# DMA transposes issued by ScalarE, and nine pairs of the first MLP's u tiles turned by them too

## The chip, the cores and the metric

One core of a Trainium2 chip runs the whole kernel. The metric is the device time of one execution in microseconds (us), as the median of several runs. The engines are TensorE (PE, with its weight loads PEld), VectorE (DVE), ScalarE (ACT), GpSimd (POOL) and SyncE (SP); each works through its own instructions in order and waits for the others by semaphores. A DMA is issued by an instruction on one engine's queue and carried out by the core's 16 DMA engines.

## The reference

A decoder trunk of two layers on 256 tokens of width 2048, in f32. Layer 0 mixes tokens by a convolution module, layer 1 by differential attention; each layer then has a squared-ReLU MLP of width 8192.

```python
def squared_relu_mlp(h, w1, b1, w2, b2):
    u = jnp.square(jax.nn.relu(h @ w1 + b1))
    return u @ w2 + b2
...
for i in range(DEPTH):
    mod = cond @ ada_w[i] + ada_b[i]
    sh_m, sc_m, g_m, sh_f, sc_f, g_f = [m[:, None, :] for m in jnp.split(mod, 6, axis=-1)]
    h = x * (1.0 + sc_m) + sh_m
    ...
    x = layer_norm(DEEPNORM_ALPHA * x + g_m * y, ln_mix_g[i], ln_mix_b[i])
    h = x * (1.0 + sc_f) + sh_f
    y = squared_relu_mlp(h, mlp_w1[i], mlp_b1[i], mlp_w2[i], mlp_b2[i])
    x = layer_norm(DEEPNORM_ALPHA * x + g_f * y, ln_ffn_g[i], ln_ffn_b[i])
```

In the attention, q and k are rotated (rope) after the product `h @ w_qkv`.

## The kernel before

**Products.** A product has the 128 tokens of a row half t (0 or 1) as its stationary side and a 512 wide strip of weights as its moving side. Every f32 value is split into a high part (a rounded copy) and a low part (the rest), and three matmuls stand for one: high by high (L702), high by low (L704), low by high (L705). A strip over 16 chunks of 128 input features is a *group*; its two row halves fill two PSUM banks. Weights arrive in tiles of 1 MB (`load_halves`, L638, SyncE's queue, four buffers `w_w`). Half of a tile, two chunks, is a *half tile*: ScalarE casts its high half `wh` (L657), VectorE subtracts to get the low half `wl` (L659), into four buffers each. One half tile feeds 12 matmuls, and a group has eight of them. `fetch` asks for half tiles four ahead (`AHEAD`), so a cast waits until TensorE has finished the half tile four places before.

**The MLP.** The width 8192 goes in four quarters q. Each quarter computes four groups g of `u` by the first weight matrix (names `w1_i_q_g`, i is the layer), then four groups by the second (`w2_i_q_n`), which take `u` as their stationary side. For that `u` must lie with features on the partitions, so each of its 512 wide tiles has to be turned. There are two ways, chosen by `by_dma(i, q, g)` for both row halves (a *pair*):

- By TensorE: ScalarE copies the PSUM bank to `us` (L1483), and two half tiles later (`U_WAIT`) four transposes per row half write `ut` (L1488). In layer 0 ScalarE adds the bias with Relu out of `ut` (L1494), four pieces per row half, and VectorE squares (L1499; in quarter 0 ScalarE, L1497); in layer 1 VectorE does both (L1501, L1504).
- By DMA (`halves_t`): ScalarE copies the bank into two planes of 16-bit halves `uh` (L1417), a DMA transposes them into `ux` (L1419), and after `T_WAIT[i]` half tiles ScalarE joins the planes to `r` (L1423); bias, Relu and square follow (L1428 on ScalarE and L1429 on VectorE in layer 0, L1431 and L1432 on VectorE in layer 1). `T_WAIT` is 6 for layer 0 and 4 for layer 1.

Both ways end in `put_split`, which makes `u_hi` (L515, ScalarE) and `u_lo` (L518, VectorE). Before the change, 13 pairs go by DMA, all in layer 1: quarters 1 to 3, and group 3 of quarter 0. The rest, 16 pairs of layer 0 and three of layer 1, go by TensorE.

**Rope.** `rope_evac` turns the rotated q and k tiles in the same manner: ScalarE makes the two planes (L1669), a DMA turns them (L1674), and four half tiles later ScalarE joins them into `qT` or `kT` (L1680). Seven pairs go this way, the last k group by TensorE (L1686).

**Beside it.** During layer 0's MLP, VectorE also computes layer 1's modulation: dot products of rows of `ada_w` with the condition (`adaw`, L230), whose 1 MB tiles share the four buffers of the weights.

**Order.** TensorE and VectorE keep the order in which the code is written. ScalarE's and SyncE's order in the MLPs and the attention is set by a scheduler, so a later step of one tile can stand ahead of an earlier step of another.

Of the kernel before, what the change touches and what calls it, by code (L numbers as in the profile page):

```python
# [82 lines left out]
def group_order(s):  # L83

    return list(range(NGRP))[::1 if (len(SLICES) - s) % 2 else -1]
# [72 lines left out]
def trunk(  # L158
# [8 lines left out]
    nc = tc.nc  # L167
# [16 lines left out]
    def tp_tile(name):  # L184
        return ps_tp[0].tile([P, 512], F32, tag="tp", name=name)
# [57 lines left out]
    def defer(n, fn):  # L243
        put_off.append((ticks[0] + n, fn))
# [265 lines left out]
    def put_split(pair, c0, n, s0, ns, src, eng=None, trail=False):  # L510

        hi, lo = pair
        h = hi[:, c0:c0 + n, s0:s0 + ns]
        l = lo[:, c0:c0 + n, s0:s0 + ns]
        nc.scalar.copy(h, src)  # L515

        def low():
            (eng or nc.vector).tensor_tensor(l, src, h.bitcast(F32), op=ALU.subtract)  # L518
        if trail:
            trailing.append(low)  # L520
        else:
            low()
# [739 lines left out]
    for s, (f0, nf) in enumerate(SLICES):  # L1262
# [6 lines left out]
        for pos, k in units:  # L1269
            g = group_order(s)[pos]  # L1270
# [3 lines left out]
            if (s, h) in X_AT:  # L1274
                a, b = X_AT[s, h]
# [8 lines left out]
            if nf > 1 or pos % 2 == 0:  # L1284
                parts = w_parts.pop(0)
# [14 lines left out]
            if not last and h >= END_AT[s]:  # L1300
                n = h - END_AT[s] - 1 + (s + 1 < BOTH_PE)
# [106 lines left out]
        defer(4 + q, lambda q=q: alpha_x(q))  # L1408

    def by_dma(i, q, g):  # L1410
        return i == 1 and (q > 0 or g == 3)

    def halves_t(t, ps, uT, i, q, g, n0):

        name = f"{i}_{q}_{g}_{t}"
        parts = work.tile([P, 2, NG], U16, tag="X", name=f"uh_{name}", bufs=3)
        nc.scalar.copy(parts, ps.bitcast(U16).rearrange("p (n b) -> p b n", b=2))  # L1417
        turned = work.tile([P, 2, 4, P], U16, tag="A", name=f"ux_{name}")
        nc.sync.dma_start_transpose(turned.rearrange("p b a n -> p (b a) n"), parts.rearrange("p b n -> p (b n)"))  # L1419

        def rest():
            r = work.tile([P, 4, P], F32, tag="B", name=f"r_{name}")
            nc.scalar.copy(r.rearrange("p a n -> p (a n)").bitcast(U16).rearrange("p (a n b) -> p a n b", a=4, b=2),  # L1423
                           turned.rearrange("p b a n -> p a n b"))
            f0 = i * 64 + n0 // P
            if i == 0:
                for j in range(4):
                    nc.scalar.activation(r[:, j, :], r[:, j, :], AF.Relu, bias=cv["b1c"][:, f0 + j:f0 + j + 1])  # L1428
                nc.vector.tensor_tensor(r, r, r, op=ALU.mult)  # L1429
            else:  # L1430
                nc.vector.tensor_tensor(r, r, cv["b1c"][:, f0:f0 + 4].unsqueeze(2).broadcast_to([P, 4, P]), op=ALU.add)  # L1431
                nc.vector.scalar_tensor_tensor(r, r, 0.0, r, ALU.max, ALU.mult)  # L1432
            put_split(uT, g * 4, 4, t * P, P, r, trail=True)
        defer(T_WAIT[i], rest)
# [218 lines left out]
    def rope_evac(nm, g, kv):  # L1653
        def on_t(t, ps):
            ph = ps.rearrange("p (h d) -> p h d", h=4)
            p1 = work.tile([P, 4, P], F32, tag="A", name=f"rp1_{nm}{g}{t}")
            nc.vector.tensor_tensor(p1.rearrange("p h (b d) -> p (h b) d", b=2),
                                    ps.rearrange("p (h d) -> p h d", d=64),
                                    at["cos"][:, t, :].unsqueeze(1).broadcast_to([P, 8, 64]), op=ALU.mult)
            p2 = work.tile([P, 4, P], F32, tag="B", name=f"rp2_{nm}{g}{t}")  # L1660
            nc.vector.tensor_tensor(p2[:, :, 0:64], ph[:, :, 64:128],
                                    at["sinN"][:, t, :].unsqueeze(1).broadcast_to([P, 4, 64]), op=ALU.mult)
            nc.vector.tensor_tensor(p2[:, :, 64:128], ph[:, :, 0:64],
                                    at["sinP"][:, t, :].unsqueeze(1).broadcast_to([P, 4, 64]), op=ALU.mult)
            nc.vector.tensor_tensor(p1, p1, p2, op=ALU.add)

            if (nm, g) != ("k", 3):
                parts = p2.rearrange("p h n -> p (h n)").bitcast(U16).rearrange("p (b n) -> p b n", b=2)
                nc.scalar.copy(parts, p1.rearrange("p h n -> p (h n)").bitcast(U16).rearrange("p (n b) -> p b n", b=2))  # L1669
                if t == 0:  # L1670
                    turned = late["pool"].tile([P, 2, 4, P], U16, tag="qkx", name=f"qkx_{nm}{g}{t}")
                else:
                    turned = work.tile([P, 2, 4, P], U16, tag="A", name=f"qkx_{nm}{g}{t}")
                nc.sync.dma_start_transpose(turned.rearrange("p b a n -> p (b a) n"),  # L1674
                                            parts.rearrange("p b n -> p (b n)"))

            def joined():
                if t == 0:
                    kv[nm] = work.tile([P, 4, S], F32, tag="X", name=f"{nm}T_{g}", bufs=3)
                nc.scalar.copy(kv[nm].bitcast(U16).rearrange("p h (n b) -> p h n b", b=2)[:, :, t * P:(t + 1) * P, :],  # L1680
                               turned.rearrange("p b h n -> p h n b"))

            def rest():
                pt = tp_tile(f"qkt_{nm}{g}{t}")
                for h in range(4):
                    nc.tensor.transpose(out=pt[:, h * P:(h + 1) * P], in_=p1[:, h, :], identity=ident)  # L1686
                if t == 0:
                    kv[nm] = work.tile([P, 4, S], F32, tag="X", name=f"{nm}T_{g}", bufs=3)
                nc.scalar.copy(kv[nm][:, :, t * P:(t + 1) * P], pt.rearrange("p (h n) -> p h n", h=4))
            if (nm, g) != ("k", 3):  # L1690
                defer(4, joined)
            else:
                defer(3, rest)
        return on_t
# [233 lines left out]
```

## Time and profile before

| | us |
|---|---|
| median of 3 runs (2267.3 to 2270.41) | 2267.64 |
| the profiled execution | 2264.22 |
| its span, first to last instruction | 2262.3 |
| TensorE's mean granted clock | 0.996 |
| DMA engines' mean busy share | 0.78 |
| mean rate of the DMA engines, GB/s | 274 |

The span falls into the convolution layer (to about 423 us), the first MLP (423 to 1070), attention with its projections (about 1100 to 1530) and the second MLP (to the end). Rows of a timeline give start, duration, engine, line, operation, output and inputs; in brackets, how long the engine stood idle before it and what ended that. A row of the group view gives busy time, mean ns of one, and after the bar the idle time before them. A matmul's row lasts longer than its place in the stream, because matmuls are pipelined: the distance between two starts is what one costs.

### The profile page before, as it was taken

The numbers are of one execution on the slowest core, as the hardware profiler recorded it, in microseconds if no ns is written. First come the engines' busy times: TensorE is split into PE (matmuls) and PEld (weight loads), VectorE is DVE, ScalarE is ACT, GpSimd is POOL, SyncE is SP. The second block draws the span as 40 slices with busy tenths as digits, with TensorE's granted clock in tenths as the row PEclk, the third lists the DMA queues.
The fourth block names the chain that finished last, engine by engine and source line by source line (L and its number), as shares of the span: only waits on it lengthen the run. The fifth ranks groups of instructions, "written<-read, shape, count | busy, mean of one in ns | idle before, by whom it ended". The sixth has DMA issues, their size and how long they took to land.

```text
span 2262.3 us, 28005 instructions
## 1 busy us (share of the span) xinstructions
PE 2223.8 (98%) x10900; PEld 1779.6 (79%) x10900; DVE 1713.5 (76%) x2124; ACT 1139.8 (50%) x1528; POOL 38.2 (2%) x53
## 2 busy tenths in 40 slices
PE   8999999999999999999999999999999999999999
PEld 5677657687888888888878788787888888888886
DVE  7688889778977888878878877887965665665567
ACT  4336773564355355355365555545444643643652
POOL 0000000000000000000000010100000000000000
PEclk9999999999999999999999999999999999999999
DMA  9996789699988888888858876875976765766773
GB/s 397 419 392 270 298 323 397 218 340 330 349 301 315 308 290 319 320 306 287 292 168 280 270 228 213 288 272 178 331 247 199 209 211 191 224 202 192 220 239 111
DMA packets 259712, 619.04 MB, mean 274 GB/s; under 512 B 52623, under 2 KB 52851, under 8 KB 230011
## 3 DMA queue, kind: packets, MB, share of 16 engines
q1 hardware_dynamic: 259580, 617.27, 77.9%
q8 instruction: 85, 1.39, 0.3%
q14 instruction: 47, 0.38, 0.0%
HBM read 604.59 MB, written 2.15 MB: 268 GB/s over the span
## 4 chain that ended last, share of the span: by engine, by line
PE 85%; DVE 7%; DMA 3%; ACT 3%; issue 1%; POOL 0%; SPq 0%; ACTq 0%; DVEq 0%; POOLq 0%
PE w_ps L704 20%; PE w_ps L705 20%; PE w_ps L702 19%; PE pw_ps L600 2%; PE pw_ps L601 2%; PE pw_ps L602 2%; PE cv L936 1%; PE pw_ps L702 1%; PE pw_ps L705 1%; PE pw_ps L704 1%; PE qkv_q_ps L705 1%; PE qkv_q_ps L702 1%; PE qkv_v_ps L704 1%; PE qkv_q_ps L704 1%; PE qkv_v_ps L705 1%
## 5 line engine op out<-in xcount | busy, mean ns | idle before, releaser
L657 ACT CAST wh_w<-w_w 128x1024 fp32r<-128x1024 f32 x512 | 535.9, 1053 | 658.1 <-PE w_ps L705 507.9
L659 DVE TENSOR_TENSOR wl_w<-w_w,wh_w 128x1024 fp32r<-128x1024 f32 x510 | 613.6, 1222 | 314.5 <-ACT wh_w L657 314.1
L702 PE MATMUL w_ps<-wh_w,hm_hi 128*128 128x512 f32 x1024 | 401.0, 392 | 2.5 <-ACT hm_hi L515 2.5
L705 PE MATMUL w_ps<-wh_w,hm_lo 128*128 128x512 f32 x1024 | 399.6, 390 | 1.6 <-DVE hm_lo L518 1.6
L704 PE MATMUL w_ps<-wl_w,u_hi 128*128 128x512 f32 x1024 | 399.1, 390 | 1.6 <-DVE wl_w L659 1.6
L702 PE MATMUL w_ps<-wh_w,u_hi 128*128 128x512 f32 x1024 | 399.1, 390 | 0.0
L704 PE MATMUL w_ps<-wl_w,hm_hi 128*128 128x512 f32 x1024 | 399.0, 390 | 0.0
L705 PE MATMUL w_ps<-wh_w,u_lo 128*128 128x512 f32 x1024 | 398.5, 389 | 0.0
L230 DVE SCALAR_TENSOR_TENSOR adaw<-adaw,cond_rows 128x2048 f32<-128x2048 f32 x108 | 246.8, 2285 | 0.2 <-DMA adaw<-in_ada_rows_dram 0.2
L702 PEld LDWEIGHTS w_ps<-wh_w,hm_hi 128*128 128x128 f32 x1024 | 192.7, 188 | 44.1 <-ACT hm_hi L515 4.1
L704 PEld LDWEIGHTS w_ps<-wl_w,u_hi 128*128 128x128 f32 x1024 | 192.3, 188 | 43.4 <-DVE wl_w L659 3.8
L705 PEld LDWEIGHTS w_ps<-wh_w,hm_lo 128*128 128x128 f32 x1024 | 192.6, 188 | 42.9 <-DVE hm_lo L518 2.9
L702 PEld LDWEIGHTS w_ps<-wh_w,u_hi 128*128 128x128 f32 x1024 | 192.3, 188 | 40.2
L704 PEld LDWEIGHTS w_ps<-wl_w,hm_hi 128*128 128x128 f32 x1024 | 192.6, 188 | 39.5
L705 PEld LDWEIGHTS w_ps<-wh_w,u_lo 128*128 128x128 f32 x1024 | 192.3, 188 | 39.8
L600 PE MATMUL pw_ps<-wh_pw,h_hi 128*128 128x512 f32 x256 | 103.9, 406 | 2.6 <-ACT wh_pw L582 1.9
L601 PE MATMUL pw_ps<-wl_pw,h_hi 128*128 128x512 f32 x256 | 100.8, 394 | 0.9 <-DVE wl_pw L585 0.8
L602 PE MATMUL pw_ps<-wh_pw,h_lo 128*128 128x512 f32 x256 | 100.5, 393 | 0.0
L585 DVE TENSOR_TENSOR wl_pw<-w_pw,wh_pw 128x1024 fp32r<-128x1024 f32 x64 | 77.3, 1221 | 28.9 <-ACT wh_pw L582 28.7
L582 ACT CAST wh_pw<-w_pw 128x1024 fp32r<-128x1024 f32 x64 | 65.9, 1051 | 44.8 <-PE pw_ps L602 25.3
L600 PEld LDWEIGHTS pw_ps<-wh_pw,h_hi 128*128 128x128 f32 x256 | 48.4, 189 | 29.6 <-issue 13.0
L518 DVE TENSOR_TENSOR u_lo<-r,u_hi 128x512 fp32r<-128x512 f32 x64 | 43.5, 689 | 28.4 <-ACT u_hi L515 28.2
(355 smaller groups left out, 3012.1 us busy)
## 6 DMA issues: line engine op xcount, KB each, us to landing
w_w<-in_mlp_w_dram SPq DMA_DIRECT2D x256, 1024.0 KB, 5.9
adaw<-in_ada_rows_dram SPq DMA_DIRECT2D x108, 1024.0 KB, 6.7
w_pw<-in_pw_tiles_dram SPq DMA_DIRECT2D x32, 1024.0 KB, 12.4
ad<-in_ada_rows_dram SPq DMA_DIRECT2D x25, 1024.0 KB, 8.5
w_pw<-in_conv_pw_w_dram SPq DMA_DIRECT2D x16, 1024.0 KB, 9.1
w_qkv_q<-in_attn_qkv_w_dram SPq DMA_DIRECT2D x16, 1024.0 KB, 5.4
w_qkv_k<-in_attn_qkv_w_dram SPq DMA_DIRECT2D x16, 1024.0 KB, 5.1
w_qkv_v<-in_attn_qkv_w_dram SPq DMA_DIRECT2D x16, 1024.0 KB, 7.1
```

What stands on the lines that cost most here:

```text
L230: nc.vector.scalar_tensor_tensor(w, w, 1.0, cond_rows, ALU.mult, ALU.mult, accum_out=m[:, ch:ch + 1])
L518: (eng or nc.vector).tensor_tensor(l, src, h.bitcast(F32), op=ALU.subtract)
L582: nc.scalar.copy(hq, rq)
L585: nc.vector.tensor_tensor(lq, rq, hq.bitcast(F32), op=ALU.subtract)
L600: nc.tensor.matmul(pss[t], lhsT=xh, rhs=wh, start=(kc == first), stop=False)
L601: nc.tensor.matmul(pss[t], lhsT=xh, rhs=wl, start=False, stop=False)
L602: nc.tensor.matmul(pss[t], lhsT=xl, rhs=wh, start=False, stop=(kc == last))
L657: nc.scalar.copy(hi, rq)
L659: eng.tensor_tensor(lo, rq, hi.bitcast(F32), op=ALU.subtract)
L702: nc.tensor.matmul(pss[tt], lhsT=xh, rhs=wh, start=(kc == 0 and job["bias"] is None), stop=False)
L704: nc.tensor.matmul(pss[tt], lhsT=xh, rhs=wl, start=False, stop=False)
L705: nc.tensor.matmul(pss[tt], lhsT=xl, rhs=wh, start=False, stop=(kc == nk - 1))
```

## The change

Two edits to the engine that issues the DMA transposes, and one to the rule that says which pairs go by DMA.

```diff
     def by_dma(i, q, g):
-        return i == 1 and (q > 0 or g == 3)
+        return i == 1 or (q > 0 and g < 3)
...
-        nc.sync.dma_start_transpose(turned.rearrange("p b a n -> p (b a) n"), parts.rearrange("p b n -> p (b n)"))
+        nc.scalar.dma_start_transpose(turned.rearrange("p b a n -> p (b a) n"), parts.rearrange("p b n -> p (b n)"))
...
-                nc.sync.dma_start_transpose(turned.rearrange("p b a n -> p (b a) n"),
-                                            parts.rearrange("p b n -> p (b n)"))
+                nc.scalar.dma_start_transpose(turned.rearrange("p b a n -> p (b a) n"),
+                                              parts.rearrange("p b n -> p (b n)"))
```

Twenty-five pairs go by DMA instead of 13: all 16 of layer 1, and nine of layer 0 (quarters 1 to 3, groups 0 to 2), whose rest is taken up six half tiles after the group instead of two. All 64 transposing DMAs, the 14 of rope among them, are issued from ScalarE's queue. TensorE has 24 rows of four transposes less.

**First place: layer 0, quarter 1, the end of group 0.** ScalarE's order before; `wh_w1_0_1_1_a_h` is the cast of half h of weight tile a of group 1, that is half tile 2a + h.

```order
L1483 COPY us_0_1_0_0_5383<-w1_0_1_0_ps0_5239 128x512
L1483 COPY us_0_1_0_1_5385<-w1_0_1_0_ps1_5240 128x512
L657 CAST wh_w1_0_1_1_1_1_5389<-w_w1_0_1_1_1_5365 128x1024
L657 CAST wh_w1_0_1_1_2_0_5436<-w_w1_0_1_1_2_5434 128x1024
L1494 ACTIVATE r_0_1_0_0_5413<-ut_0_1_0_0_5408,vec1_101 128x128 x4
L1494 ACTIVATE r_0_1_0_1_5425<-ut_0_1_0_1_5420,vec1_101 128x128 x4
L515 CAST u0_1_hi_5237<-r_0_1_0_0_5413 128x4x128
L657 CAST wh_w1_0_1_1_2_1_5452<-w_w1_0_1_1_2_5434 128x1024
L515 CAST u0_1_hi_5237<-r_0_1_0_1_5425 128x4x128
```

ScalarE's order there after the change:

```order
L1417 COPY uh_0_1_0_1_5387<-w1_0_1_0_ps1_5240 128x1024
L657 CAST wh_w1_0_1_1_1_1_5393<-w_w1_0_1_1_1_5365 128x1024
L1419 DMA_TRANSPOSE ux_0_1_0_0_5385<-uh_0_1_0_0_5383 128x8x128
L1419 DMA_TRANSPOSE ux_0_1_0_1_5389<-uh_0_1_0_1_5387 128x8x128
L657 CAST wh_w1_0_1_1_2_0_5414<-w_w1_0_1_1_2_5412 128x1024
L657 CAST wh_w1_0_1_1_2_1_5430<-w_w1_0_1_1_2_5412 128x1024
L1423 COPY r_0_1_0_0_5483<-ux_0_1_0_0_5385 128x1024
L1423 COPY r_0_1_0_1_5491<-ux_0_1_0_1_5389 128x1024
L1428 ACTIVATE r_0_1_0_0_5483<-r_0_1_0_0_5483,vec1_101 128x128 x4
L657 CAST wh_w1_0_1_1_3_0_5448<-w_w1_0_1_1_3_5446 128x1024
L1428 ACTIVATE r_0_1_0_1_5491<-r_0_1_0_1_5491,vec1_101 128x128 x4
L657 CAST wh_w1_0_1_1_3_1_5464<-w_w1_0_1_1_3_5446 128x1024
```

Two issues stand between the casts of half tiles 3 and 4, and two joining copies between those of 5 and 6; the casts of `u_hi` move behind the cast of half tile 9.

**Second place: VectorE for the same pair, after the change.** Before it, the squares and `u_lo` stood ahead of the low half of tile 2 (`wl_w1_0_1_1_2_0`).

```order
L659 TENSOR_TENSOR wl_w1_0_1_1_3_1_5465<-w_w1_0_1_1_3_5446,wh_w1_0_1_1_3_1_5464 128x1024
L230 SCALAR_TENSOR_TENSOR adaw_1_1_13_5468,mod_1_1_4639<-adaw_1_1_13_5468,cond_rows_108 128x2048
L1429 TENSOR_TENSOR r_0_1_0_0_5483<-r_0_1_0_0_5483 128x512
L1429 TENSOR_TENSOR r_0_1_0_1_5491<-r_0_1_0_1_5491 128x512
L518 TENSOR_TENSOR u0_1_lo_5238<-r_0_1_0_0_5483,u0_1_hi_5237 128x4x128
L518 TENSOR_TENSOR u0_1_lo_5238<-r_0_1_0_1_5491,u0_1_hi_5237 128x4x128
L659 TENSOR_TENSOR wl_w1_0_1_2_0_0_5504<-w_w1_0_1_2_0_5501,wh_w1_0_1_2_0_0_5503 128x1024
```

The four operations on `r` now stand between the low halves of half tiles 7 and 8.

**Third place: layer 1, quarter 1, the end of group 0.** ScalarE after the change; before it, the same rows stood in the same order without the two transposes, which were on SyncE's queue ahead of a load of weights.

```order
L1417 COPY uh_1_1_0_0_14007<-w1_1_1_0_ps0_13869 128x1024
L1417 COPY uh_1_1_0_1_14011<-w1_1_1_0_ps1_13870 128x1024
L657 CAST wh_w1_1_1_1_1_1_14017<-w_w1_1_1_1_1_13989 128x1024
L1419 DMA_TRANSPOSE ux_1_1_0_0_14009<-uh_1_1_0_0_14007 128x8x128
L1419 DMA_TRANSPOSE ux_1_1_0_1_14013<-uh_1_1_0_1_14011 128x8x128
L657 CAST wh_w1_1_1_1_2_0_14035<-w_w1_1_1_1_2_14033 128x1024
L1423 COPY r_1_1_0_0_14067<-ux_1_1_0_0_14009 128x1024
L1423 COPY r_1_1_0_1_14072<-ux_1_1_0_1_14013 128x1024
L657 CAST wh_w1_1_1_1_2_1_14051<-w_w1_1_1_1_2_14033 128x1024
```

The two issues stand between the casts of half tiles 3 and 4, ahead of the joining copies that wait for them.

## The prediction

> **What bounds the kernel now.** First the page: busy time by engine, then the chain that ended last.
>
> ```profile
> PE 2223.8 (98%) x10900; PEld 1779.6 (79%) x10900; DVE 1713.5 (76%) x2124; ACT 1139.8 (50%) x1528; POOL 38.2 (2%) x53
> PE 85%; DVE 7%; DMA 3%; ACT 3%; issue 1%; POOL 0%; SPq 0%; ACTq 0%; DVEq 0%; POOLq 0%
> ```
>
> TensorE is the bound. A matmul that waits for nothing is worth its place in the stream, so next comes the list of what TensorE waited for (total us, times, longest):
>
> ```profile
> PE w_ps L704 <- DVE wl_w L659: 1.6, 4, 0.6
> ...
> PE qkv_k_ps L704 <- DVE wl_qkv_k L659: 1.1, 1, 1.1
> PE qkv_v_ps L704 <- DVE wl_qkv_v L659: 0.9, 1, 0.9
> ```
>
> Over two MLPs and the qkv products TensorE waits 3.6 us for split weights. Fewer instructions on TensorE therefore shorten the run one to one, as long as ScalarE (which casts the high halves) and VectorE (the low halves) stay ahead.
>
> **What is removed.** Each pair of u tiles (one group, both row halves) costs TensorE eight transposes. TensorE's timeline in the first MLP, second quarter:
>
> ```profile
> 658.01 0.39 PE L704 MATMUL w_ps<-wl_w,hm_hi 128*128 128x512 f32 x1
> 658.24 0.39 PE L705 MATMUL w_ps<-wh_w,hm_lo 128*128 128x512 f32 x1
> 658.47 1.03 PE L1488 MATMUL ut<-ident,us 128*128 128x128 f32 x8
> 659.26 0.48 PE L702 MATMUL w_ps<-wh_w,hm_hi 128*128 128x512 f32 x1
> 659.58 0.40 PE L704 MATMUL w_ps<-wl_w,hm_hi 128*128 128x512 f32 x1
> ```
>
> Matmuls start every 0.227 us (658.24 less 658.01 is 0.23; twelve of them, a half tile, take 2.72). From 658.24 to 659.58 are 1.34 us; without the eight it would be two steps, 0.45. A pair costs **0.89 us**. By the order of instructions 24 rows of four transposes go, that is 12 pairs: nine in the first MLP, three in the second. 12 x 0.89 = **10.7 us**, all on the path.
>
> **What is added and moved.** The operations exist in the second MLP already (tile and group views; min/median/max in ns, landing in us from issue):
>
> ```profile
> L1419 SPq DMA_TRANSPOSE ux<-uh x26: 1238/1276/4808, 1641.6 to 2166.5; - x26
> DMA to landing us min/median/max: 3.1/3.3/4.1
> L1674 SPq DMA_TRANSPOSE qkx_q<-rp_q x8: 1232/1238/1347, 1179.9 to 1399.5; - x8
> DMA to landing us min/median/max: 3.0/3.2/6.1
> L1417 ACT COPY uh<-w_ps 128x1024 uint16<-128x1024 uint16 x26 | 25.1, 1016 | 12.2 <-PE w_ps L705 12.2
> L1423 ACT COPY r<-ux 128x1024 uint16<-128x1024 uint16 x26 | 29.9, 1169 | 3.1 <-DMA ux<-uh 3.0
> L1483 ACT COPY us<-w_ps 128x512 f32<-128x512 f32 x38 | 21.8, 585 | 16.1 <-PE w_ps L705 14.8
> ```
>
> An issue held SyncE's queue 1.25 us. No row shows one on ScalarE. One end is nothing (the queue issues while the engine still runs the cast ahead of it), the other the full 1.25 us; I take the full time, the nearest row. ScalarE then gets 64 x 1.25 = 80 us of issues (26 + 14 moved, 24 new), and 24 x (1016 - 585 + 1169 ns) = 38 us of copies. 1140 + 118 us is 56% of the span: as an average it fits, so the question is the half tiles just after a group ends.
>
> **First MLP, after group (1,0).** ScalarE and VectorE before:
>
> ```profile
> 632.60 1.27 ACT L1483 COPY us<-w_ps 128x512 f32<-128x512 f32 x2 [0.98 <-PE w_ps L705]
> 633.76 1.05 ACT L657 CAST wh_w<-w_w 128x1024 fp32r<-128x1024 f32 x1
> 637.39 1.05 ACT L657 CAST wh_w<-w_w 128x1024 fp32r<-128x1024 f32 x1 [2.58 <-DMA w_w<-in_mlp_w_dram]
> 638.35 2.16 ACT L1494 ACTIVATE r<-ut,vec 128x128 f32<-128x128 f32 x8
> ...
> 630.07 2.29 DVE L230 SCALAR_TENSOR_TENSOR adaw<-adaw,cond_rows 128x2048 f32<-128x2048 f32 x1
> 639.51 0.69 DVE L1499 TENSOR_TENSOR r<-r 128x512 f32<-128x512 f32 x1 [1.23 <-ACT r L1494]
> 643.13 2.35 DVE L659 TENSOR_TENSOR wl_w<-w_w,wh_w 128x1024 fp32r<-128x1024 f32 x2
> ```
>
> The group ends at 633.1; half tile j of the next starts at 633.1 + 2.72 j, and its weight buffers (four) come free 2.72 x (j - 3) after 633.1. Now the new order on the same clock: copies to 634.6, cast 3 to 635.6, two issues to 638.1, casts 4 and 5 to 640.2, the two joining copies to 642.5 (landed at 635.6 + 3.3 = 638.9 and 636.9 + 3.3 = 640.2), Relu and casts 6 and 7 to 646.8, cast 8 to 647.9. Cast 9 waits for its buffer until 649.4. VectorE: low half 7 to 648.1, an ada product to 650.4, two squares to 651.8; the two u_hi casts and u_lo end at 653.1, low half 8 at 654.3. TensorE needs that at 633.1 + 8 x 2.72 + 0.23 = 655.1. **Cover 0.8 us**, plus the 1.1 us by which the second landing (640.2) is early for its copy (641.3): nothing stalls until a landing takes about 5.2 us. The six half tiles matter here: the squares stand behind low half 7, where before VectorE waited for them (1.23 us) ahead of low half 4.
>
> What can lengthen a landing is the traffic (windows: PE, PEld, DVE, ACT, POOL busy, clock, DMA share, GB/s):
>
> ```profile
> 615.00:715.00 100.00, 100.00 (x459) 83.07 (x458) 77.78 (x77) 52.95 (x84) 0.00 (x0) 1.00 0.85 295
> 1769.00:1770.00 1.00, 1.00 (x6) 0.84 (x5) 0.00 (x0) 0.62 (x1) 0.00 (x0) 1.00 1.01 393
> 1774.00:1775.00 1.00, 1.00 (x6) 0.84 (x5) 0.72 (x1) 0.47 (x2) 0.00 (x0) 1.00 1.02 190
> ```
>
> With loads alone full engines move 393 GB/s, with transposes in flight 190. At that rate 256 KB take about 1.4 us (estimate), a pair 2.8 us, 13% of a group's 21.8 us on top of a share of 0.85: close to full. If all nine pairs landed as late as the 6.1 us seen in the qkv stage, nine stalls of 0.9 us make 8 us; if none, 0. I take **1.5 us**, two pairs of nine, since 6.1 is the worst of fourteen.
>
> **Second MLP, 13 moved pairs and three new ones.** Here the rest comes four half tiles later, and the row of SyncE shows the issues that move:
>
> ```profile
> 1771.38 1.93 ACT L1417 COPY uh<-w_ps 128x1024 uint16<-128x1024 uint16 x2 [0.95 <-PE w_ps L705]
> 1773.19 1.06 ACT L657 CAST wh_w<-w_w 128x1024 fp32r<-128x1024 f32 x1
> 1774.78 1.06 ACT L657 CAST wh_w<-w_w 128x1024 fp32r<-128x1024 f32 x1 [0.53 <-PE w_ps L705]
> 1775.74 2.31 ACT L1423 COPY r<-ux 128x1024 uint16<-128x1024 uint16 x2
> 1777.95 1.05 ACT L657 CAST wh_w<-w_w 128x1024 fp32r<-128x1024 f32 x1
> ...
> 1772.42 2.61 SPq L1419 DMA_TRANSPOSE ux<-uh  x2
> 1775.54 15.61 SPq L638 DMA_DIRECT2D w_w<-in_mlp_w_dram  x4
> ...
> 1779.03 1.23 DVE L659 TENSOR_TENSOR wl_w<-w_w,wh_w 128x1024 fp32r<-128x1024 f32 x1 [1.94 <-ACT wh_w L657]
> 1785.15 3.49 DVE L659 TENSOR_TENSOR wl_w<-w_w,wh_w 128x1024 fp32r<-128x1024 f32 x3
> ```
>
> The group ends at 1772.0. Issued behind the cast, the transposes start at 1774.25 and 1775.5, not at 1772.42; cast 4 ends at 1777.9, the joining copies at 1780.2, cast 5 at 1781.2, low half 5 at 1782.5, VectorE's four passes over r (2.7 us) at 1785.2, two u_lo at 1786.8, low half 6 at 1788.0. TensorE needs it at 1772.0 + 6 x 2.72 + 0.23 = 1788.5. **Cover 0.5 us**, or 1.5 where an issue overlaps the cast. A landing of 4.1 us, the longest of 26, overruns by 0.3. Ends: 0 and 16 x 0.3 = 5 us; I take **0.5**.
>
> **Rope, 14 moved transposes.** In the new order the copy that waits for the first landing stands ahead of the second issue, so ScalarE falls some 3.5 us behind per pair (2.5 us of issues, about 1 of landing). Its cover is TensorE's lead of three half tiles, 8.2 us, less one cast and one low half (2.3 us); but VectorE is loaded there, and two of the three waits quoted above fall in this stage, at about 1 us. Ends: 0 and seven pairs at 0.7; I take **1.2 us**.
>
> **SyncE** no longer waits for ScalarE's copies:
>
> ```profile
> SPq L1419 <- ACT uh L1417: 46.8, 12, 4.0
> ```
>
> But the load behind them (1775.54) starts when VectorE frees its buffer (the low half that ends at 1775.5), so I count nothing; at most the 3.6 us of weight waits could go.
>
> **Sum.** 10.7 - 1.5 - 0.5 - 1.2 = 7.5 us less. The profiled execution took 2264.2 us (span 2262.3 and 1.9 around it): 2256.7. The median of the runs is 2267.64, 3.4 us above it, so **2260.1 us** as a median.
>
> **Rivals.**
> 1. *The gain is eaten* (within 0.2%, 4.5 us, about what a measurement here tells from no change). Stalls of 6.2 to 15 us: a mean of 0.25 to 0.6 us per MLP pair, 25 pairs. For it: covers of 0.5 and 0.8 us, one issue of 4.8 us in 26. Against: the largest stalls are worst cases taken everywhere. At 0.43 us per pair the time is 2267.6. Chance 0.17.
> 2. *Slower: ScalarE's in-order queue waits on its own transposes.* Place: the joining copy, with the next weight cast queued behind it, VectorE behind that, TensorE last. If issues hold ScalarE fully and landings stretch by 1.5 us beyond the median, the second MLP stalls 1.0 us per pair, the first about as much with its traffic: 25 - 10.7 = 14 us more, 2282. It decides from 0.6 us per pair. Against: SyncE's ring shows a median of 3.3 us beside the same loads. Chance 0.12.
> 3. *A transpose by DMA is simply the dearer one, and its time shows.* If the whole way (two issues and a landing, 5.8 us) came into TensorE's path at the 12 new pairs: 12 x (5.8 - 0.89) = 59 us more, 2327. Against: 13 pairs take this way already, and weight waits in total are 1.6 us. Chance 0.02. [...]
> 4. *More than the sum*: stalls vanish with SyncE freed, 10.7 + 3.6 = 14.3 us less, 2253.3. Chance 0.04.
>
> The forecast itself (4.6 to 10.7 us less) has 0.65. **Range**: from 2254 (nearly rival 4) to 2271 (all ends of the unknown costs together, 8 + 5 + 5 - 10.7 = 7, are 2275, and I leave that tail out with the slower rivals, some 0.15). Faster 0.69, same 0.17, slower 0.14.
>
> **What would show it.** Right: 56 transposes left at L1488; groups of the first MLP 21.8 us apart instead of 22.7; waits of TensorE for wl_w under 6 us in total; ScalarE's joining copies without idle time for ux. Wrong: idle time of ScalarE before them in microseconds, landings over 5 us in the first MLP, or weight casts that no longer wait for TensorE.

## The result, and the profile after

The changed kernel takes 2360.1 us (median of 4 runs, 2358.55 to 2365.21), the kernel before 2268.59 in the same job: a ratio of 1.0407, 95% interval 1.0388 to 1.0426. The forecast was 2260.1, with a range to 2271; the result is some 92 us slower than before.

The page of the profiled execution after the change (a span of 2356.5 us against 2262.3): busy time of the engines, the granted clock and the rate of the DMA engines in 40 slices, and the two DMA rings.

```profile
PE 2247.9 (95%) x10804; PEld 1784.8 (76%) x10804; DVE 1711.9 (73%) x2124; ACT 1174.2 (50%) x1552; POOL 40.4 (2%) x53
...
PEclk9999999999988999999999999999999999999999
DMA  9995899598988999899849777784986766765773
GB/s 397 420 383 218 334 343 390 201 358 320 313 234 251 317 305 283 324 323 262 306 149 286 245 227 182 252 310 156 275 264 204 216 206 196 215 207 189 219 221 109
...
q1 hardware_dynamic: 217340, 606.78, 73.9%
q10 hardware_dynamic: 67584, 16.79, 5.2%
```

TensorE does 96 instructions fewer, yet is busy for longer: 2247.9 us against 2223.8. It also stands idle for 108.6 us of the span instead of 38.5. The 94.2 us between the spans are thus 70.1 of idle time and 24.1 of busy time; with the forecast's 10.7 us less work, the lower clock (0.978 on average, 0.996 before) costs about 35, an estimate (24.1 + 10.7). q1 is SyncE's ring, with all loads; q10 is new, ScalarE's ring with the 64 transposes, 1056 packets each (67584 / 64).

TensorE's and ScalarE's waits after the change, and the tile `ux` with its transposes (columns of a wait: total us, times, longest):

```profile
PE w_ps L702 <- ACT wh_w L657: 38.0, 8, 11.7
PE w_ps L704 <- DVE wl_w L659: 20.9, 22, 3.1
PE qkv_k_ps L704 <- DVE wl_qkv_k L659: 12.4, 2, 9.9
```

```profile
ACT r L1423 <- DMA ux<-uh: 77.9, 20, 11.3
...
ACT wh_w L657 <- issue: 24.5, 6, 7.2
```

```profile
L1419 ACTq DMA_TRANSPOSE ux<-uh x50: 1247/1350/7399, 638.1 to 2252.7; - x50
...
DMA to landing us min/median/max: 3.2/5.5/22.9
```

TensorE now waits for the weights' high halves, which it did not do in the MLPs before: ScalarE, which makes them, stands for 77.9 us in front of joining copies whose transposes have not landed (3.0 us before), and for 24.5 us behind issues of its own that take up to 7.4 us. A landing takes up to 22.9 us; on SyncE's ring, before, the longest was 4.1 us. The view times only some of the landings, 13 of 50 here and 12 of 26 before.

The first new pair shows the chain. ScalarE's timeline in the first MLP, after the change, then TensorE's one row with an idle time there:

```profile
637.08 1.93 ACT L1417 COPY uh<-w_ps 128x1024 uint16<-128x1024 uint16 x2 [0.98 <-PE w_ps L705]
638.12 1.34 ACTq L1419 DMA_TRANSPOSE ux<-uh  x1
638.89 1.07 ACT L657 CAST wh_w<-w_w 128x1024 fp32r<-128x1024 f32 x1
639.51 4.89 ACTq L1419 DMA_TRANSPOSE ux<-uh  x1
644.52 2.00 ACT L657 CAST wh_w<-w_w 128x1024 fp32r<-128x1024 f32 x2 [4.56 <-issue]
648.51 1.18 ACT L1423 COPY r<-ux 128x1024 uint16<-128x1024 uint16 x1 [1.99 <-DMA ux<-uh]
660.63 1.16 ACT L1423 COPY r<-ux 128x1024 uint16<-128x1024 uint16 x1 [10.94 <-DMA ux<-uh]
```

```profile
663.96 0.79 PE L702 MATMUL w_ps<-wh_w,hm_hi 128*128 128x512 f32 x1 [9.91 <-ACT wh_w L657]
```

The second issue holds ScalarE for 4.9 us, the second joining copy waits for 10.9, no cast gets past it, and TensorE stands for 9.9. The windows around it (columns: window, its length, busy time of PE, PEld, DVE, ACT and POOL with instructions, granted clock, DMA share, GB/s):

```profile
632.00:640.00 8.00, 8.00 (x37) 6.64 (x36) 4.58 (x5) 4.99 (x5) 0.00 (x0) 1.00 0.84 296
640.00:648.00 8.00, 8.00 (x37) 6.60 (x37) 5.79 (x5) 2.00 (x2) 0.00 (x0) 1.00 1.22 157
648.00:656.00 8.00, 6.04 (x27) 4.68 (x25) 0.00 (x0) 1.18 (x1) 0.00 (x0) 1.00 1.16 91
656.00:664.00 8.00, 0.04 (x1) 0.05 (x1) 0.07 (x1) 3.37 (x7) 0.00 (x0) 0.51 0.72 267
664.00:672.00 8.00, 7.53 (x22) 5.66 (x23) 6.97 (x8) 5.14 (x9) 0.00 (x0) 0.64 0.54 188
```

While both rings have work the DMA engines' records overlap (a share over 1), yet they move only 91 to 157 GB/s, where the kernel before has 208 to 356 in the same stretch. The records of single packets show how: from 651.9 to 652.7 twelve load packets of 8 KB start that last 4.9 to 5.5 us each, to 657.0 to 657.6, where the median of that size is 0.31. After the stop TensorE's granted clock is 0.51 (656 to 664), and products whose rows last 0.39 us before (a mean of 0.390 to 0.392) last 0.79.

Where the time went, by stages, each from its first product to that of the next, in us. The landmarks are the first row of `w_ps` with `hm_hi`, with `u_hi`, of `qkv_q_ps`, and so on, and the last stage ends with the span; the pieces before the first MLP and at `wo` differ by 3 us or less between all profiles:

| | before | after | difference | pairs by DMA there, before and after |
|---|---|---|---|---|
| first MLP, quarter 0, first weights | 96.8 | 96.7 | -0.1 | 0, 0 |
| the rest of the first MLP | 627.3 | 677.9 | +50.6 | 0, 9 |
| q, k, v, rope, attention | 298.4 | 315.4 | +17.0 | 7, 7 |
| second MLP, quarter 0, first weights | 97.1 | 113.8 | +16.7 | 1, 4 |
| the rest of the second MLP | 621.3 | 629.0 | +7.7 | 12, 12 |

### The profile page after: what moved, and what is told of

Same layout as the page of the kernel before. It is cut to its first block, busy times and chain, and to the rows that moved or that the text cites. A ratio compares the mean times of both kernels' runs of the same rounds, so it can differ in the third digit from the quotient of the medians.

```text
span 2356.5 us, 27901 instructions
## 1 busy us (share of the span) xinstructions
PE 2247.9 (95%) x10804; PEld 1784.8 (76%) x10804; DVE 1711.9 (73%) x2124; ACT 1174.2 (50%) x1552; POOL 40.4 (2%) x53
## 3 DMA queue, kind: packets, MB, share of 16 engines
q10 hardware_dynamic: 67584, 16.79, 5.2%
## 5 line engine op out<-in xcount | busy, mean ns | idle before, releaser
L702 PE MATMUL w_ps<-wh_w,hm_hi 128*128 128x512 f32 x1024 | 408.4, 399 | 40.0 <-ACT wh_w L657 38.0
L704 PE MATMUL w_ps<-wl_w,hm_hi 128*128 128x512 f32 x1024 | 407.6, 398 | 13.5 <-DVE wl_w L659 13.5
L705 PE MATMUL w_ps<-wh_w,hm_lo 128*128 128x512 f32 x1024 | 405.7, 396 | 1.6 <-DVE hm_lo L518 1.6
L1423 ACT COPY r<-ux 128x1024 uint16<-128x1024 uint16 x50 | 57.2, 1169 | 77.9 <-DMA ux<-uh 77.9
## 6 DMA issues: line engine op xcount, KB each, us to landing
w_pw<-in_pw_tiles_dram SPq DMA_DIRECT2D x32, 1024.0 KB, 13.3
```

The costliest lines, as they stand in the source:

```text
L702: nc.tensor.matmul(pss[tt], lhsT=xh, rhs=wh, start=(kc == 0 and job["bias"] is None), stop=False)
L704: nc.tensor.matmul(pss[tt], lhsT=xh, rhs=wl, start=False, stop=False)
L705: nc.tensor.matmul(pss[tt], lhsT=xl, rhs=wh, start=False, stop=(kc == nk - 1))
```

## The experiments

The change has two parts: more transposes by DMA, and another ring for all of them. Two explanations offer themselves: the second ring does it, by slow landings and long issues in the queue of the engine that casts the weights; or the added transposes do it, on whichever ring. The first runs take one part each. In the expectations the letters of the theories are each run's own.

**The twelve pairs on SyncE's ring.** The kernel before with the changed rule only:

```diff
     def by_dma(i, q, g):
-        return i == 1 and (q > 0 or g == 3)
+        return i == 1 or (q > 0 and g < 3)
```

> The rule of the change (25 pairs by DMA, 64 transposes), but all transposes issued from SyncE's queue as before the change. Theory A (two queues: the transposes on ScalarE's own queue are interleaved with the weight loads on the DMA engines, and both crawl): landings fall back to 3 to 6 us, TensorE waits under 10 us in total, median 2258 to 2263 us. Theory B (the issuing instruction costs ScalarE its time): the same, 2258 to 2263. Theory C (24 more transposes are too much for ScalarE, VectorE or the DMA engines, on whichever queue): landings over 10 us in the first MLP and at least 2300 us.

Measured: 2275.14 us against 2265.68, ratio 1.004 (1.0025 to 1.0055). All three theories missed the time, though landings fell nearly as A has it. So the ring makes some 82 of the 92 us, but the forecast's gain does not come on SyncE's ring either: the nine pairs of the first MLP change its rest by -0.3 us, the three of the second MLP add 7.1 to its first stage. ScalarE's wait for `ux` in this run:

```profile
  DMA ux<-uh: 22.2, 15
...
DMA to landing us min/median/max: 3.2/4.7/8.2
```

Landings beside the loads of the first MLP, as far as they are timed, are 3.6 to 8.2 us even here, not 3.3.

**ScalarE's ring with the old 13 pairs.** The changed kernel with the rule of before:

```diff
     def by_dma(i, q, g):
-        return i == 1 or (q > 0 and g < 3)
+        return i == 1 and (q > 0 or g == 3)
```

> The old rule (13 pairs by DMA, 40 transposes), all issued from ScalarE's queue. Theory A: the first MLP is as before the change to 1 us (no transposes there); loss only where adaw loads run beside transposes, in rope and in quarter 0 of the second MLP, by the trace of the change some 20 to 35 us of stalls: 2285 to 2305 us. Theory B: loss in proportion to the issues, 40 of 64 of 92 us: about 2325 us, spread over quarters 1 to 3 of the second MLP too. Theory C: within 0.3% of before.

Measured: 2286.61 us, ratio 1.0088 (1.0062 to 1.0115). Moving the rope's seven pairs and the 13 old ones costs 20 us without a single new transpose: 11.6 in the attention, 5.5 in the rest of the second MLP. The time is theory A's, the places only in part: quarter 0 of the second MLP lost nothing, and the second figure, which A did not expect there, is one event, at 2181.2 us: an issue of 6.6 us with three casts behind it. It is the MLP's last pair, and SyncE had just issued two loads of 1 MB for the final layer norm (`fin`, L1807, at 2179.3 and 2179.7). In the kernel before, the same two loads stand ahead of the same pair, and its issue on SyncE is the 4.8 us of the prediction's row. Alone, the ring costs 20 us and the added pairs on SyncE's ring 9.5; together they cost 92. At the pair worked out in the prediction (cover 0.5 us) TensorE does not wait.

**No wait for the landing.** The changed kernel, in which the first and second MLP's joining copy reads the planes as they were before turning; the transposes still run:

```diff
             nc.scalar.copy(r.rearrange("p a n -> p (a n)").bitcast(U16).rearrange("p (a n b) -> p a n b", a=4, b=2),
-                           turned.rearrange("p b a n -> p a n b"))
+                           parts.rearrange("p b (a n) -> p a n b", a=4))
```

> The change, but the joining copy in the MLPs (L1423) reads the untransposed planes, so nobody waits for a landing; the transposes are still issued from ScalarE's queue and run beside the loads (the turning of these tiles is left out of the result). Theory A with the wait for the landing as the main cost: the 78 us in which ScalarE stood idle for ux go, and most of TensorE's stalls with them: 2275 to 2305 us, the rest from loads that arrive late and from rope. Theory B: ScalarE is still held by 50 issues of 1.3 to 7.4 us: at least 2340 us.

Measured: 2331.1 us against 2265.68, ratio 1.0288 (1.0261 to 1.0314), between the two expectations. 65 us of the loss remain: the wait before the joining copies is worth some 26 of the 92 us and no more. ScalarE's timeline of this run at the same pair:

```profile
636.13 2.25 ACTq L1419 DMA_TRANSPOSE ux<-uh  x1
636.90 1.06 ACT L657 CAST wh_w<-w_w 128x1024 fp32r<-128x1024 f32 x1
638.42 8.16 ACTq L1419 DMA_TRANSPOSE ux<-uh  x1
646.70 1.04 ACT L657 CAST wh_w<-w_w 128x1024 fp32r<-128x1024 f32 x1 [8.74 <-PE w_ps L705]
```

With no landing waited for, the issue itself holds ScalarE for 8.2 us. The bracket names TensorE, which is the last event by the profile; but the issue ends at 646.58 and the cast starts right behind it. The loads come no later in sum than before the change (`wh_w` waits 127.3 us for them, 129.4 before; 89.0 in the changed kernel), but up to 12.4 us late at once, where it was 6.7.

**Smaller rows of the other loads.** The modulation tiles of the second layer (and one set of the first), 1 MB each in rows of 8 KB per partition, laid out in four strips with rows of 2 KB, like the weights; the same in the kernel before as a control:

```diff
...
-            nc.sync.dma_start(w, ada_rows[ADA_ROWS[i, v, ch]])
+            nc.sync.dma_start(w.rearrange("p (a n) -> p a n", a=4),
+                              ada_rows[ADA_ROWS[i, v, ch]].rearrange("p n -> (p n)").rearrange(
+                                  "(a p n) -> p a n", a=4, p=P))
```

> The change, with the 1 MB adaw tiles laid out in the inputs so that one contiguous piece is 2 KB like that of the weights, instead of 8 KB. Theory A in its form by packets (the engines take turns between the two queues packet by packet, so a transpose of small pieces waits for one large packet after each of its own): landings in the first MLP fall from 11 to 23 us to 4 to 7, and the time to 2265 to 2300 us. Theory A by sheer load (the bytes of adaw saturate the engines): landings and time stay, 2345 us or more.

> The kernel before with the modulation tiles of the second layer (and one of the first) laid out in 2 KB pieces: the control of the changed kernel with the same edit, which took 2339.65. If the smaller rows cost nothing without a second ring, 2262 to 2272, and the 20 us that they saved in the changed kernel are the second ring's; if they slow the loads by themselves, up to 2285, and they saved more.

Measured: 2339.65 us for the changed kernel (ratio 1.0325, 1.0282 to 1.0369) and 2268.98 for the control (1.0005, 0.9996 to 1.0015). The rows cost nothing without a second ring; with it they are worth about 18 us (two runs, 15 us apart), and 72 to 74 remain, between the two theories. Landings in the first MLP are still 5.3 to 14.9 us. No load packet lasts over 3 us any more, where the changed kernel has 72 such, so the long packets are not the main part of the loss.

**Without the modulation loads.** GpSimd fills the tile instead of the DMA, in the changed kernel and in the kernel before:

```diff
-            nc.sync.dma_start(w, ada_rows[ADA_ROWS[i, v, ch]])
+            nc.gpsimd.memset(w, 0.25)
```

> The changed kernel without the modulation loads of the second layer (108 of 1 MB from the first MLP on): GpSimd fills the buffers with a constant instead, so that these modulations are not those of the reference. Read against the same edit of the kernel before. Theory A (the transposes suffer from the loads that run beside them): with the weight loads alone, as in the second MLP's last quarters, landings in the first MLP fall from a median of 8 to 16 us to under 5 us, and the difference between the two kernels with this edit shrinks from 92 to under 30 us. Theory B (ScalarE's own order, joining copies before casts, does it whatever else runs): the difference stays at 60 us or more.

> The kernel before, with the same modulation loads left out (GpSimd writes a constant): the control of the run beside it. TensorE is the bound, so 2245 to 2270 us by both theories; if GpSimd's fills (108) delay VectorE, up to 2300.

Measured: 2278.61 and 2265.13 us: the difference between the two kernels falls from 92 to 13.5, as theory A of this pair has it. `ux` in the changed kernel without those loads:

```profile
  DMA ux<-uh: 16.6, 9
...
DMA to landing us min/median/max: 3.2/3.5/7.2
```

What is gone is the traffic beside the transposes: the rest of the first MLP moves 205 GB/s instead of 292. It then takes 624.4 us, 1.0 less than its control; the second MLP holds what is left, 5.5 and 7.2 us.

**The rings by themselves.** Two kernels with data movement alone. In the first, nothing held the transposes in their stages:

> The whole computation is left out; the kernel only moves data, in stages one after the other, so its time as a whole means nothing. 1 MB weight loads into six buffers: 'full' (each buffer freed at once), 'pace' (VectorE holds each buffer for four subtractions of 1.2 us, so about one load in 5 us, 210 GB/s, as in the first MLP), 'big' (full, with rows of 8 KB instead of 2 KB). Each is run without transposes, with two 128x1024 transposes behind every fourth load on SyncE (sp), and the same on ScalarE (act). 'both' has the loads alone, on SyncE and ScalarE in turn. 'xs' and 'xa' are eight transposes alone. Theory A (two rings with work at one time cost throughput): sp lowers full from some 350 to about 270 GB/s (16 transposes at 1.9 us of all engines, the share of ScalarE's ring in the changed kernel), act to 150 or less, and landings in act are 10 us or more, in paceact too; xs and xa are alike at 3.2 us. Theory B (a transpose costs the DMA engines the same wherever it is issued): act equals sp within 10% everywhere. Theory C (ScalarE issues or completes its transposes more slowly by itself): xa is slower than xs by 1 us or more a piece. If any two rings do it, both falls under 250 GB/s; if it takes a transposing ring, both stays near full.

Only its stages `fullsp` and `fullact` can be read; the transposes of the later ones ran ahead of their loads, and those meant to run alone ran beside the first loads. In the two, sixteen transposes beside 32 loads of 2 KB rows cost the same total on either ring: the loads are issued over 104 us with SyncE's transposes (114.5 to 218.6) and over 102 with ScalarE's (231.9 to 334.3). So theory B of this run, the same cost on either ring, fits these two stages; the 150 GB/s of theory A did not show, it was 232 to 251 at worst. On SyncE's ring, with loads ahead of them in the same ring, the transposes are slow as well:

```profile
L215 SPq DMA_TRANSPOSE fullsp_u<-parts x16: 3394/5634/8692, 119.0 to 228.4; - x16
DMA to landing us min/median/max: 5.4/9.0/13.3
```

The second kernel ties each pair to a loaded tile:

```python
    if ring is not None and k % every == every // 2:
        for j in range(2):
            ...
            nc.scalar.copy(pt.rearrange("p a n -> p (a n)"), t[:, j * NG:(j + 1) * NG].bitcast(U16))
            ...
            eng.dma_start_transpose(u.rearrange("p b a n -> p (b a) n"), pt.rearrange("p b n -> p (b n)"))
            ...
    for _ in range(slow):
        nc.vector.tensor_tensor(wide[:, 0:1024], t[:, 0:1024], t[:, 1024:2048], op=ALU.subtract)
```

> As the run with data movement alone (the whole computation is left out, its time as a whole means nothing), but with every transpose held in its place by its data: ScalarE copies the 128x1024 planes from a loaded tile and two transposes of them follow, once in eight loads, which is the traffic of the first MLP (four buffers of 1 MB, each held by VectorE for two subtractions of 1.2 us; in the slow stages for four). twok: strips of 2 KB; eight: rows of 8 KB; mix: in turn. Each alone or with transposes on SyncE (sp) or ScalarE (act); peact is mixact with TensorE at work. 32 loads of a stage take 87 us at the 387 GB/s that the first run showed, and eight transposes at the 1.5 us that it showed 12 us more. Theory A1 (it is the second ring that collapses the DMA engines): mixact and twokact take over 125 us, mixsp and twoksp under 105, landings over 10 us on ScalarE and 5 to 8 on SyncE. Theory A2 (it is the rows of 8 KB of the modulation loads beside a second ring): only mixact and eightact do, twokact stays under 105. Theory B (a transpose costs the same on either ring, and what is slow in the changed kernel comes from its engines waiting for each other): all stages with transposes take 95 to 105 us. The slow stages tell whether spare time of the DMA engines heals it: 24 loads at 5 us, 120 us, with landings of 4 us.

Measured, with the time from VectorE's first to its last subtraction of a stage, and the landings of the eight transposes in it (six in the slow stages), in us. In `peact` TensorE's products ran ahead of the stage, so it only repeats `mixact`:

| loads beside them | no transposes | on ScalarE | landing | on SyncE | landing |
|---|---|---|---|---|---|
| rows of 2 KB | 86.0 | 98.8 | 8.4 to 17.8 | 105.8 | 3.1 to 3.9 |
| in turn | 81.2 | 120.9 (again 121.5) | 10.5 to 28.4 | 104.7 | 3.1 to 3.9 |
| rows of 8 KB | not run | 142.2 | 7.4 to 34.8 | 94.7 | 3.1 to 3.9 |
| in turn, a load in 5 us | not run | 119.7 | 4.1 to 4.6 | 119.7 | 4.0 to 4.7 |

The issue and landing rows of `mixact`, `mixsp` and `slowact`, three fences:

```profile
L211 ACTq DMA_TRANSPOSE mixact_u<-mixact_h x8: 1247/3576/10269, 413.9 to 517.6; - x8
DMA to landing us min/median/max: 10.5/18.1/28.4
```

```profile
L211 SPq DMA_TRANSPOSE mixsp_u<-mixsp_h x8: 1243/1262/1281, 548.7 to 630.0; - x8
DMA to landing us min/median/max: 3.1/3.2/3.9
```

```profile
L211 ACTq DMA_TRANSPOSE slowact_u<-slowact_h x6: 1248/1632/2150, 910.0 to 992.0; - x6
DMA to landing us min/median/max: 4.1/4.4/4.6
```

That is nearest to A2, and none of the three as written: on the second ring both the landing and the issue stretch, and the time grows with the rows. With rows of 2 KB the stage stays under 105 us and is even shorter than on SyncE; with both kinds it takes 120.9, short of the 125 of both theories. In the slow stages, with the DMA engines at 0.70 (ScalarE) and 0.68 (SyncE) of their time, the two rings do not differ. On SyncE the transposes land in 3.2 us, not in the 5 to 8 of A1: SyncE stands until their planes are written, which are copied from the tile loaded last, so no load is ahead of them by then (from 549.2 to 549.8, ahead of the first pair in `mixsp`, the rate of the DMA engines is 0 to 1 GB/s). With loads ahead it was 5.4 to 13.3 (`fullsp`). The price of standing is the loads that wait behind, 20 to 24 us for eight beside rows of 2 KB and of both kinds.

What the two rings do is seen in the packets of four microseconds of `mixact` (429 to 433), and of five of the stage with rows of 8 KB on ScalarE (667 to 672; packets, MB, share):

```profile
q1 hardware_dynamic: 358, 1.11, 92.8%
q10 hardware_dynamic: 358, 0.09, 10.9%
```

```profile
DMA  0101001040010110301103011061030910590900
...
q1 hardware_dynamic: 66, 0.52, 27.5%
q10 hardware_dynamic: 68, 0.02, 2.3%
```

358 and 358, 66 and 68 (21 and 20 before the next load starts at 671): in these stretches either ring starts about as many packets as the other, though a packet has some 250 bytes on the transposing ring (0.09 MB over 358) and 2 or 8 KB on the other (3.1 KB as a mean of the 358, 7.9 KB of the 66). In three more stretches of 4 us of `mixact`, from 417 to 429, q1 and q10 have 304 and 260, 441 and 490, 293 and 291. The records of single packets look like turns of one packet each: from 667.15 on a packet of q10 (18 ns) and one of 8 KB of q1 (309 ns) follow each other every 0.32 us. Spread evenly over the 16 engines a transpose has 66 packets on each (1056 / 16); at 0.33 us for a load packet of the second fence (27.5% of 5 us of 16 engines, by 66) that is 22 us, an estimate; its median landing is 24.1. The row of tenths shows the other loss: hardly a packet starts before 671. It counts a packet where it starts, so it leaves out thirteen load packets of 8 KB that start at 664.0 to 664.1 and last 6.6 to 6.9 us, all to 670.6 or 671.0. They end nearly together; what they wait for was not tested. This stage has 80 load packets of over 3 us, `peact` 14, and the others none.

**Can the nine pairs pay on SyncE's ring?** The old 13 pairs and nine of the first MLP:

```diff
     def by_dma(i, q, g):
-        return i == 1 and (q > 0 or g == 3)
+        return (i == 1 and (q > 0 or g == 3)) or (i == 0 and q > 0 and g < 3)
```

> The kernel before with the nine added pairs of the first MLP (quarters 1 to 3, groups 0 to 2) turned by DMAs on SyncE, and the old 13 pairs of the second MLP kept: 22 pairs. Theory A (on one ring the nine pairs break even, and the three added pairs of the second MLP's first quarter lost 7 us in the run with 25 on SyncE): 2264 to 2269 us, the ratio 0.998 to 1.001. Theory B (the nine pairs lose as well, through later loads): 2272 or more. The working of the prediction (nine pairs at 0.89 us each with no stall): 2259.6.

Measured: 2266.11 us, ratio 0.9996 (0.9985 to 1.0006), no difference. The rest of the first MLP as one window, before and then with 22 pairs:

```profile
520.50:1147.80 627.30, 624.90 (x2814) 516.78 (x2812) 508.17 (x549) 294.66 (x400) 0.54 (x1) 1.00 0.86 308
```

```profile
521.60:1146.20 624.60, 618.16 (x2742) 509.06 (x2741) 506.44 (x548) 322.46 (x418) 0.54 (x1) 1.00 0.92 317
```

TensorE's busy time falls by 6.7 us, its idle time (length less busy) rises from 2.4 to 6.4, and 2.7 us are left. ScalarE waits 17.7 us at eight joining copies there. Two runs tried to win these back by taking the copies up later. First by a copy of one column on VectorE ahead of each joining copy, taken up four half tiles after the group:

```diff
-T_WAIT = (6, 4)
+T_WAIT = (4, 4)
...
             r = work.tile([P, 4, P], F32, tag="B", name=f"r_{name}")
+            if i == 0:
+                nc.vector.tensor_copy(r[:, 0, 0:1], split[-1][-1][1][:, 0:1].bitcast(F32))
```

> The same 22 pairs on SyncE, but the first MLP's joining copies are held back: a one-column copy on VectorE, from the low half of the weight tile split last, goes ahead of each, and the joining step is taken up four half tiles after the group's end, so that ScalarE comes to it about 11 us behind the issue instead of about 5. Theory A (on one ring what is lost is that ScalarE waits at a joining copy taken up before its transpose lands): the idle time of ScalarE before these copies falls from 22 us to under 3, and the time is 2258 to 2264, faster than the kernel before by 2 to 9 us. Theory B (the loads behind the transposes are late, whoever waits): no change against the run with 22 pairs and no delay, within 2 us.

Measured: 2332.85 us, ratio 1.0288 (1.0274 to 1.0302). Both theories missed. ScalarE's wait at all its joining copies fell from 22.9 us to 5.3, nearly as meant, but VectorE's squares kept their early places:

```profile
DVE r L1431 <- ACT r L1430: 76.6, 18, 6.4
```

18 waits of 4.3 us in the queue that makes the low halves, and the stage is 69 us longer than with 22 pairs alone. Then with both moved: the joining copies pinned behind a cast three half tiles after the group (`nc.scalar.copy` of one column of `wh`), the squares two half tiles later, pinned behind a low half (`nc.vector.scalar_tensor_tensor` of one column):

> 22 pairs on SyncE, the first MLP's joining copies held back again, now on both engines: ScalarE's own one-column copy from a weight tile's high half pins the joining copies behind the cast three half tiles after the group's end, and VectorE's squares follow two half tiles later, pinned behind that low half. In the run with the copies held back alone VectorE, whose order was not moved, waited 77 us for r in 18 places. Theory A (that wait was its whole loss, and the early joining copies are what eats the gain of 22 pairs): VectorE's wait for r under 5 us, ScalarE's idle time before the joining copies under 5 us instead of 23, 2256 to 2263, ratio 0.995 to 0.998. Theory B (the late loads behind the transposes eat the gain, whoever waits): 2264 to 2270, as with 22 pairs. If the pins cost more than they save: over 2270.

Measured: 2277.2 us, ratio 1.0046 (1.0034 to 1.0059). VectorE's wait for `r` is gone, ScalarE's is 15.7 us still, the loads are waited for longer (`wh_w` 156.2 us, 135.5 with 22 pairs, 129.4 before) and TensorE's waits for `wl_w` rise from 5.4 to 14.2. The pins cost more than they save. No version here beats the kernel before.

## Why the prediction was wrong

- **What bounds the kernel**: right. TensorE is the bound, and what happened came to it through waits for weights.
- **The work removed, 10.7 us**: right in kind, somewhat large. 56 transposes are left at L1488 (152 before), as forecast; the nine pairs take 6.7 us out of TensorE's busy time in the run with 22 pairs on SyncE, 0.75 us each and not 0.89.
- **The nine new pairs, +1.5 us, "nothing stalls until a landing takes about 5.2 us"**: this is the step that failed. The landing put into the threshold was 3.3 us, the median of SyncE's ring in the second MLP, where the weights alone are loaded. On ScalarE's ring in the first MLP landings are 3.5 to 22.9 us, and the stage grows by 50.6 us: 41.8 more idle time of TensorE, and 8.8 more busy time, as the 15.5 us (8.8 and the 6.7 of work removed) that are put down to the lower clock (0.97 in this stage, 1.00 before; 0.50 in five stretches of 41.0 us in all) outdo the work removed. By the records of single packets, TensorE stands 0 to 2.1 us after the three pairs whose second transpose was written within 5.6 us of its issue, and 2.1 to 12.1 us after the six where that took 10.8 to 22.4: the threshold is not refuted, the landing is. The worst cases behind the upper ends were not known to be the worst: the 4.1 and the 6.1 us, called the longest of 26 and of fourteen, are those of the 12 and the 5 landings that the view times. With what was to be saved there (8.0) the term is near 59 us, not 1.5; its upper end was 8. It is already too small on SyncE's ring with 22 pairs, where the landings timed are 5.2 to 6.7 us and TensorE's idle time grows by 4.
- **Rope, +1.2 us (to 5)**: 17.0, of which the run with 13 pairs shows 11.6 for the ring alone. In the changed kernel the three landings that are timed take 4.0, 7.8 and 17.0 us, and TensorE waits 12.4 us for the k weights.
- **The second MLP, +0.5 us (to 5)**: 27. In quarter 0, beside the last modulation loads, 16.7 us more instead of 2.7 less. In quarters 1 to 3, with weight loads alone, the working held: the landings timed are 3.2 to 4.2 us, and TensorE does not wait at the pair that was worked out. The 5.5 to 7.7 us there come from the last pair alone, behind the two loads of `fin`: its second issue takes 6.6 to 7.2 us on ScalarE, a term that was taken as 1.25 us. The row it was taken from has the same pair as its longest, 4.8 us on SyncE, where no cast stands behind it.
- **SyncE set free**: nothing was gained by it, as forecast.
- **The rivals**: rival 2 named the mechanism and the place rightly, the joining copy with the casts queued behind it. It priced it at 25 us of stalls for a landing 1.5 us beyond the median, and gave it 0.12 since SyncE's ring "shows a median of 3.3 us beside the same loads". A ring that waits its turn behind all loads in its own queue says nothing about one that shares the engines with them. Nor is the joining copy's wait all of it: taking that wait away gave back some 26 of 92 us; the long issues, the late loads and the rope hold the rest, in proportions that no run separates. Rival 3, the whole way at each new pair, was 33 us too small; the old pairs and the rope, which it leaves out, make 20 by the run with 13 pairs.
- **TensorE or a DMA for the turning**: TensorE does it no dearer here even against SyncE's ring, where 12 more pairs by DMA cost 9.5 us and nine gain nothing (a ratio of 0.9996). On ScalarE's ring the cause is not its price per tile but the traffic beside it: without the modulation loads 78 of the 92 us go. On SyncE's ring no run took the traffic away.

What stays open: in the changed kernel, from 644 to 648 us, q10's packets took 54 ns each as a mean (1131 in 4 us, 94.5% of the engines' time). Most of them last 18 ns (1011 at most 20), while 66 of 0.3 us and more hold nearly two thirds of the time. From 648.5 to 650.5 they start in bursts 0.32 us apart, which is also the step of the load packets of 8 KB (0.31 to 0.32 us each, two at a time). That engines with no load left keep pace with the slowest one is the author's guess, which no run tests; why load packets of 8 KB stay open so long was not tried either. The stage that was to run beside TensorE's products did not, so whether work on the engines slows the transposes is open too.

## What to carry to other kernels

A duration read from one DMA queue holds for that queue and the traffic beside it; before a DMA with many small packets goes to a second queue, ask how full the engines are there, for a landing that took 3.3 us (the median) on SyncE's ring in the second MLP took as much as 22.9 us on ScalarE's in the first, with the engines 0.86 busy before. One queue is no shelter by itself: behind loads in the same ring it was 5.4 to 13.3. ScalarE stood for 24.5 us behind its own issues, for 7.2 us at once, so none belongs in the queue of an engine that the bound waits for, unless the longest issue seen fits into its cover. And where the DMA engines are at 0.9 of their time, work moved from a bound engine to a DMA can come back as waits: here 6.7 us of work became 4.0 of idle time.

## What the runs showed of the hardware

- With two rings on the same engines, in four stretches of 4 us of `mixact` (417 to 433), the loads' ring and the transposes' started 304 and 260 packets, 441 and 490, 293 and 291, 358 and 358, so packets of some 250 bytes came on no faster there than those of 2 and 8 KB. Landings of two transposes have medians of 12.3, 18.1 and 24.1 us beside rows of 2 KB, both, and 8 KB, against 3.2 us on the loads' own ring with no load ahead, and 9.0 there with loads ahead.
- The issue of a DMA transpose took 1.2 us at its shortest and, on ScalarE's ring beside loads, up to 8.2 us in the kernels and 12.9 us in the stage with rows of 8 KB. On SyncE's ring it stretched too: 3.4 to 8.7 us with loads ahead (`fullsp`), against 1.2 to 1.3 with none (`mixsp`). Behind two loads of 1 MB the last pair's took 6.4 to 7.2 us on ScalarE, 4.2 to 5.8 on SyncE.
- Beside transposes on a second ring some load packets of 8 KB stayed open for over 3 us instead of 0.31: 72 did in the changed kernel, up to 7.5 us, and 80 in the stage with rows of 8 KB on ScalarE, up to 8.8. None did in the kernels with SyncE's ring alone, and none where the modulation loads have rows of 2 KB or are left out.
- At that first pair TensorE's granted clock fell to half 2 us after its last product (654.0 to 656.1) and came back 5.7 us after the next (664.0 to 669.7). In the rest of the first MLP five stops, with longest idle times of 2.1 to 11.7 us, were followed by such a stretch, and stops of 1.4 us and less were not. The five stretches are 41.0 us long, with TensorE busy for 24.4 of them, half of which is lost by the clock of 0.50: some 12 us, an estimate, against the 15.5 by the busy times, on top of 41.8 us of added idle time.
